# Two norms' right halves in a pipeline, and the gates among five pairs of products

## The chip, the cores and the metric

The kernel runs on one core of a Trainium2 chip. The engines of the core that matter here are TensorE (PE, matrix products), VectorE (DVE), ScalarE (ACT), GpSimd (POOL) and SyncE (SP, which starts the loads of weights). Each engine works through its own list of instructions in order, and waits where an instruction needs what another engine or a transfer has not yet delivered. The metric is the device time of one execution in microseconds (us).

## The reference

One layer of a diffusion backbone on 640 tokens (128 of context, 512 of latents) with 1024 channels: a SwiGLU half step, a mixer, a second half step, a last norm. Each of the first three stages begins with a norm that is modulated by channel, differently for the two token groups:

```python
def rmsnorm(x, g):
    y = x32 * lax.rsqrt(jnp.mean(x32 * x32, axis=-1, keepdims=True) + EPS)
    return (y * g.astype(jnp.float32)).astype(x.dtype)

    h = modulate(rmsnorm(x, norm_g[0]), sh1, sc1)
    x = x + 0.5 * g1[:, None, :] * swiglu(h, ffn1_w1, ffn1_w2)
    h = modulate(rmsnorm(x, norm_g[1]), shm, scm)
    y, C, n, m = mixer(h, ...)
    x = x + gm[:, None, :] * y
    h = modulate(rmsnorm(x, norm_g[2]), sh2, sc2)
    x = x + 0.5 * g2[:, None, :] * swiglu(h, ffn2_w1, ffn2_w2)
```

The mixer multiplies h by one wide matrix; of its columns come q, k, v, o, the mLSTM's input and forget gates, and two sets of merge gates. The mLSTM needs cumulated sums of log-sigmoids of the forget gates and running maxima, in both directions, before its first chunk:

```python
    z = h @ w_in + b_in
    ...
    b = jnp.cumsum(lfc, axis=-1)
    dmat = jnp.where(causal, b[..., :, None] - b[..., None, :] + ic[..., None, :], -jnp.inf)
    m_t = jnp.maximum(a, jnp.max(dmat, axis=-1))
    ...
    ml = (o * hm) @ w_ml_out
    sc = (bg * uc) @ w_sc_out
    y = jax.nn.sigmoid(z[..., GML_OFF:GSC_OFF]) * ml + jax.nn.sigmoid(z[..., GSC_OFF:IN_COLS]) * sc
```

## The kernel before, in words

**Products.** Everything is float32; a product of two float32 matrices is made of three products of reduced parts (`three`: high times high, high times low, low times high). Of each weight tile ACT makes the high part (wh, L73, a cast) and DVE the low part (wl, L74, a subtraction). The tokens lie in two halves of 320 columns, left and right. Most large products are done in *pairs* of 128 output rows by a scheme with seven products instead of eight (`pair_steps`). A pair's seven products P0 to P6 have 12 matmuls of 128x320 each. They need sums of weights (ws, L213, DVE) and combinations of the activations (H11, H12, HT1 to HT4 and so on). Between them stand small steps: a copy of the first bank by ACT after P0 (L268), copies by ACT after P1, P2 and P4 (L274, L278, L286), additions by DVE (L287 after P4, L292 after P5). P2 needs the copy L268, P4 needs L278, P6 needs L286, and the next pair's P1 needs L292 of this one. What a pair delivers last is handled late: it is flushed behind the next pair's L268.

**Norms two and three.** The norm stands ahead of a `head_el`: a loop over eight k steps in which three blocks of the left half are multiplied side by side (nine matmuls a step), followed by the three blocks' right half and the remaining blocks. The left half's rows are made while the stage before ends (`halves_el` and `left_lists`, seven lists of work that `after_lists` calls one by one). The right half's norm is made while the left half is multiplied: `chain[0]` is the statistics (the sum over channels of the squares, a matmul L719 of `sqacc` with ones; ACT's square root, DVE's reciprocal and three diagonals), `chain[1]` the spread of the result over all partitions by matmuls (L736), the scales of the eight rows (`scale_x`, L744, DVE) and the first four modulates (`modulate`, L752 on ACT or L754 on DVE in turn), `chain[2]` the other modulates and the splits (L73 cast by ACT, L74 subtraction by DVE) of the first four rows into HT4, `chain[3]` those of the last four into H22. Norm three's right half shares ACT with two silus of the second half step (L854), which need another table of functions.

**Gates.** After the first of the mixer's products, 38 steps of `gates()` (cumulated sums and maxima on DVE, exponentials and a logarithm on ACT, some transfers by POOL) and one step that opens buffers are dealt out evenly over pairs by `weave`: a step is put behind a product as soon as its share is reached. The four pairs are the last of v, the first of the merge gates gml (its results go through a sigmoid, L1516), and two of q and k. ACT holds one table of functions at a time, and where a function of another table follows, an ACT_TABLE_LOAD stands ahead of it.

**Later stages.** The other merge-gate pairs lie further on: gml's second pair among the first head's steps, its third and fourth beside the norm of the mLSTM's output, the four of gsc behind the ml stage.

Of the kernel before, what the change touches and what calls it, by code (L numbers as in the profile page):

```python
# [14 lines left out]
KT = 8  # L15
# [29 lines left out]
def mixer_step(ctx: ExitStack, tc: tile.TileContext, x_prompt, x_sample, state_C, state_n, state_m,  # L45
# [131 lines left out]
    def step(fn):  # L177
        return element([], [], fn)
# [147 lines left out]
    def plain_acts(k, h):  # L326
        if h == 0:
            return HB["11" if k < 4 else "21"][k % 4]
        return HB["12" if k < 4 else "22"][k % 4]

    def head_el(blocks, chain, work, mid=()):


        pre, nb = len(mid) // 2, len(blocks)
        order = [None] * pre + [0, 1, 2] + [None] * (len(mid) - pre) + list(range(3, nb))
        points = 4 * nb - 6
        at_ = {t: i for i, t in enumerate(order) if t is not None}

        def emit():
            flush()  # L340
            n = {"i": 0}

            def take(u, i):
                u["emit"](raw(el["base"] + i))
                rdone.add(el["base"] + i)
                load_more()

            def some(*_):
                n["i"] += 1
                if n["i"] == 3 and soon:  # L350
                    soon.pop(0)()
                while len(work) > 0 and n["i"] * total >= points * (total - len(work) + 1):
                    work.pop(0)()

            total = len(work)
            ev = lambda t: lambda h_, ps: blocks[t][1](h_, ps)
            hold()
            for i in range(pre):
                take(mid[i], i)
            w = [[op()] for t in range(3)]  # L360
            ps = [big() for t in range(3)]
            for k in range(KT):
                if k == 4:
                    for t in range(3):
                        w[t].append(op())
                for t in range(3):
                    three(ps[t][:, :HT], *w[t][k // 4], k % 4, plain_acts(k, 0), k == 0, k == KT - 1)
                if k == 3:
                    chain[0]()
                if k == 4:  # L370
                    chain[1]()
            for t in range(3):
                ev(t)(0, ps[t][:, :HT])
            chain[2]()
            for i in range(pre, len(mid)):
                take(mid[i], 3 + i)
            chain[3]()
            for t in range(3):
                unit(w[t], KT, plain_acts, 1, ev(t), {3: some, 7: some})
                release(2)  # L380
            for t in range(3, nb):
                w = [op(), op()]
                unit(w, KT, plain_acts, 0, ev(t), {3: some, 7: some})
                unit(w, KT, plain_acts, 1, ev(t), {3: some, 7: some})
            while work:
                work.pop(0)()
            for f in chain[4:]:
                f()
        loads = [b[0] for b in blocks]
        loads = [u["raws"][0] for u in mid[:pre]] + loads[:3] + [u["raws"][0] for u in mid[pre:]] + loads[3:]  # L390
        oa = [dict(tile_ops(KT, at_[t])[i], raws=[at_[t]]) for i in range(2) for t in range(3)]
        ob = [dict(o, raws=[at_[t]]) for t in range(3, nb) for o in tile_ops(KT, at_[t])]
        el = dict(element(loads, oa + ob, emit), calm=True)
        return el

# [382 lines left out]
    def right_chain(n, sh):  # L778

        def all_of(*fs):  # L780
            def f():
                for x in fs:
                    x()
            return f

        def scales():
            for k in range(KT):
                scale_x(1, k, N["rb", 1])

        def mods(ks):  # L790
            for k in ks:
                modulate(1, k, n, sh, "AV"[k % 2])

        def right(ks):
            for k in ks:
                if k < 4:
                    HB.setdefault("12", [None] * 4)[k] = hl = hpair("T4")
                    split(N[1, k], *hl)
                else:
                    put("22", k - 4, N[1, k])  # L800

        def t1(k):
            N["T", k] = utile()
            V.tensor_sub(N["T", k], N[1, k], N[0, k])

        def t2(k):
            V.tensor_sub(N["T", k], N[1, k + 4], N["T", k])

        def t3_(k):
            V.tensor_sub(N[1, k], N[1, k + 4], N[1, k])  # L810

        def t4(k):
            V.tensor_sub(N["T", k], N[0, k + 4], N["T", k])
        ks = range(4)
        work = [lambda k=k: t1(k) for k in ks] + [lambda k=k: put("T1", k, N["T", k]) for k in ks]
        work += [lambda k=k: t3_(k) for k in ks] + [lambda k=k: put("T3", k, N[1, k]) for k in ks]
        work += [lambda k=k: t2(k) for k in ks] + [lambda k=k: put("T2", k, N["T", k]) for k in ks]
        work += [lambda k=k: t4(k) for k in ks]
        last = [lambda k=k: put("T4", k, N["T", k]) for k in ks]
        chain = [stat_fn(1), all_of(rows_fn(1), scales, lambda: mods(range(4))),  # L820
                 all_of(lambda: mods(range(4, 8)), lambda: right(range(4))), lambda: right(range(4, 8))]
        return chain + last, work

    def add_x(m, h, ps, g, last):
# [56 lines left out]
    def after_lists(n, sh):  # L881
        lists = left_lists(n, sh)

        def after(h, i):
            if h == 1:
                for f in lists[i]:
                    f()
                if i == 5:
                    for f in lists[6]:
                        f()  # L890
        return after


# [628 lines left out]
    def cx_pair(m):  # L1522
        def ev(mi, h, src):
# [25 lines left out]
            for o, i in segs:  # L1549
# [7 lines left out]
    prog += [step(spill_x), step(close_u), step(open_h1)]  # L1557
    gate, NG = gates(), 38
    h1 = head_q(1)
    prog += weave([pair_el(*j, spare_v=True) for j in (h0[2], gml_pair(0), h1[0], h1[1])],  # L1560
                  [step(lambda: next(gate, None))] * NG + [step(open_ml)])
    for h in range(NH):
        o_pair = q_pair(h, "o", O_OFF)
        if h == 0:
            jobs = [gml_pair(2), h1[2], o_pair]
        elif h + 1 < NH:
            jobs = head_q(h + 1) + [o_pair]
        else:
            jobs = [cx_pair(0), o_pair, cx_pair(1)]
        prog += weave([pair_el(*j) for j in jobs], head_steps(h))  # L1570
# [114 lines left out]
    rs += [n_out, lambda: None, open_m2]  # L1685
    rs += [lambda j=j: (r_in(j)(), r_load(j + 3)() if j + 3 < KT else None) for j in range(KT)]
    rs = [step(f) for f in rs]
    prog += weave([pair_el(*gml_pair(m), spare_v=True) for m in (4, 6)], rs)
    ml = [plain_el(w_load(w_ml_out, 0, KT, m * P, D), KT, lambda k, h: RB[k, h], ml_ev(m)) for m in range(KT)]
    for m in range(KT):  # L1690
        ml[m]["fill"] = [step(g_load(m + 1))] if m + 1 < KT else []
# [2 lines left out]
    for m in range(0, KT, 2):  # L1694
        if m:
            prog += [pair_el(*cx_pair(m), G), pair_el(*cx_pair(m + 1), G)]
        prog.append(pair_el(*bg_pair(m), G, spare_v=True))
    prog += weave([pair_el(*gsc_pair(m)) for m in range(0, KT, 2)], [step(lambda: None)] * 3 + [step(t_in(0))])
    y_acts = lambda k, h: YB[k, h]
    sc = [plain_el(w_load(w_sc_out, 0, KT, m * P, D), KT, lambda k, h: PB[k, h], sc_ev(m)) for m in range(KT)]  # L1700
    for m in range(KT - 1):
# [102 lines left out]
```

## Time and profile before

| | |
|---|---|
| median of 3 runs | 1712.4 us (1710.86 to 1714.94) |
| profiled execution | 1714.5 us |
| its span on the core | 1712.7 us |
| granted TensorE clock, mean | 0.994 |
| busy: PE, DVE, ACT, POOL | 1673.4, 1269.8, 798.3, 166.5 us |
| pairs of the gates | 541 to 591 us |
| norm two's right half | 501 to 520 us |
| norm three's right half | 1256 to 1277 us |

A row of the profile's time line gives the start in us, the duration, the engine, the line and the operation, output and inputs, and in brackets how long the engine stood idle just before and who released it. A row of the windows gives busy us of each engine in the stretch, then PE's granted clock and the share and rate of the transfers. The matmul durations overlap: one starts about every 0.15 us though each is listed with 0.31.

### The profile page before, as it was taken

How to read it: one execution, taken by the hardware profiler on the slowest of the kernel's cores; microseconds unless marked ns; L12 is line 12 of the kernel's file. 1: busy time of each engine (PE TensorE's matmuls, PEld its weight loads, DVE VectorE, ACT ScalarE, POOL GpSimd, SP SyncE). 2: the span in 40 equal slices, each digit the busy share in tenths (PEclk: the TensorE clock that was granted, in tenths of full speed). 3: DMA queues.
4: the chain of work that ended last, by engine and by line, in shares of the span. 5: the costliest groups of instructions: out<-in, count | busy, mean ns of one | idle time of the engine just before them, and what ended most of it. 6: DMA issues, size and time to landing. Idle time of an engine off the chain costs nothing.

```text
span 1712.7 us, 29519 instructions
## 1 busy us (share of the span) xinstructions
PE 1673.4 (98%) x11269; PEld 1625.6 (95%) x11269; DVE 1269.8 (74%) x2684; ACT 798.3 (47%) x1719; POOL 166.5 (10%) x250
## 2 busy tenths in 40 slices
PE   7999999999999899999999999999999999999997
PEld 4989999999989899999999999999989999999997
DVE  6767786886778867777887788879677567566576
ACT  4542451542456666465662355542265335244253
POOL 2010000000030231111111221011100000000002
PEclk9999999999999999999999999999999999999999
DMA  9344334333352443333348433357432322323222
GB/s 310 86 144 140 99 109 118 110 112 108 102 159 75 107 105 84 84 100 83 95 144 270 120 83 83 96 167 214 123 99 65 96 62 84 90 74 90 84 74 62
DMA packets 278349, 193.14 MB, mean 113 GB/s; under 512 B 12291, under 2 KB 256650, under 8 KB 278208
## 3 DMA queue, kind: packets, MB, share of 16 engines
q1 hardware_dynamic: 268960, 161.96, 32.8%
q0 software_dynamic: 8480, 28.63, 5.9%
q8 instruction: 89, 1.46, 0.3%
q10 hardware_dynamic: 768, 0.66, 0.1%
q14 instruction: 52, 0.43, 0.1%
HBM read 175.92 MB, written 15.31 MB: 112 GB/s over the span
## 4 chain that ended last, share of the span: by engine, by line
PE 83%; DVE 8%; ACT 5%; issue 3%; DMA 1%; POOL 0%; ACTq 0%; DVEq 0%; POOLq 0%
PE ps L240 25%; PE ps L242 25%; PE ps L241 25%; DVE wl L74 2%; PE ax L1385 1%; PE ax L1416 1%; ACT wh L73 1%; PE ax L636 1%; PE ax L1388 1%; PE ax L561 1%; DVE ws L213 1%; DVE t L1529 1%; DMA wr<-in_ffn_w_dram 0%; DVE x L1541 0%; PE ax L1362 0%
## 5 line engine op out<-in xcount | busy, mean ns | idle before, releaser
L74 DVE TENSOR_TENSOR wl<-wr,wh 128x512 fp32r<-128x512 f32 (+1 forms) x410 | 266.9, 666 | 81.1 <-ACT wh L73 79.5
L73 ACT CAST wh<-wr 128x512 fp32r<-128x512 f32 (+1 forms) x410 | 238.7, 593 | 181.3 <-PE ps L241 152.5
L74 DVE TENSOR_TENSOR wl<-ws,wh 128x512 fp32r<-128x512 f32 x288 | 203.0, 705 | 62.4 <-ACT wh L73 62.0
L73 ACT CAST wh<-ws 128x512 fp32r<-128x512 f32 x288 | 175.2, 618 | 111.6 <-DVE ws L213 65.9
L240 PE MATMUL ps<-Uh,wh 128*128 128x320 f32 x704 | 218.5, 310 | 0.0
L241 PE MATMUL ps<-Ul,wh 128*128 128x320 f32 x704 | 217.3, 309 | 0.0
L242 PE MATMUL ps<-Uh,wl 128*128 128x320 f32 x704 | 217.2, 308 | 0.0
L828 DVE SCALAR_TENSOR_TENSOR x<-ps,modT,x 128x128 f32<-128x128 f32 (+2 forms) x216 | 82.7, 433 | 121.1 <-PE ps L242 121.1
L241 PEld LDWEIGHTS ps<-Ul,wh 128*128 128x128 f32 x704 | 132.1, 188 | 0.2 <-DVE Ul L74 0.2
L240 PEld LDWEIGHTS ps<-Uh,wh 128*128 128x128 f32 x704 | 132.1, 188 | 0.0
L242 PEld LDWEIGHTS ps<-Uh,wl 128*128 128x128 f32 x704 | 132.1, 188 | 0.0
L240 PE MATMUL ps<-HT4h,wh 128*128 128x320 f32 x384 | 122.4, 319 | 8.5 <-DVE t L289 3.5
L240 PE MATMUL ps<-H11h,wh 128*128 128x320 f32 x384 | 121.1, 315 | 2.0 <-ACT H11h L73 2.0
L240 PE MATMUL ps<-H21h,wh 128*128 128x320 f32 x384 | 120.3, 313 | 1.2 <-ACT H21h L73 1.2
L241 PE MATMUL ps<-HT4l,wh 128*128 128x320 f32 x384 | 119.8, 312 | 0.2
L242 PE MATMUL ps<-HT4h,wl 128*128 128x320 f32 x384 | 119.6, 312 | 0.0
L241 PE MATMUL ps<-H11l,wh 128*128 128x320 f32 x384 | 119.0, 310 | 0.6 <-DVE H11l L74 0.4
L242 PE MATMUL ps<-H21h,wl 128*128 128x320 f32 x384 | 119.1, 310 | 0.3
L241 PE MATMUL ps<-H21l,wh 128*128 128x320 f32 x384 | 118.7, 309 | 0.1
L242 PE MATMUL ps<-H11h,wl 128*128 128x320 f32 x384 | 118.6, 309 | 0.0
L240 PE MATMUL ps<-H22h,wh 128*128 128x320 f32 x352 | 110.6, 314 | 0.0
L242 PE MATMUL ps<-H22h,wl 128*128 128x320 f32 x352 | 109.1, 310 | 0.0
(399 smaller groups left out, 4531.1 us busy)
## 6 DMA issues: line engine op xcount, KB each, us to landing
wr<-in_ffn_w_dram SPq DMA_DIRECT2D x86, 512.0 KB, 3.9
wr<-in_w_in_dram SPq DMA_DIRECT2D x72, 512.0 KB, 3.9
wr<-in_w_mod_dram SPq DMA_DIRECT2D x64, 512.0 KB, 4.0
wr<-in_ffn_w_dram SPq DMA_DIRECT2D x48, 384.0 KB, 3.5
wr<-in_ffn_w_dram SPq DMA_DIRECT2D x20, 256.0 KB, 3.0
early<-in_w_mod_dram SPq DMA_DIRECT2D x8, 512.0 KB, 9.1
wr<-in_w_ml_out_dram SPq DMA_DIRECT2D x8, 512.0 KB, 5.1
wr<-in_w_sc_out_dram SPq DMA_DIRECT2D x8, 512.0 KB, 4.2
```

Of the source, the lines that this page charges most:

```text
L73: A.copy(hi, raw)
L74: V.tensor_sub(lo, raw, f32(hi))
L213: getattr(engine, fn)(t, part(o, a), part(o, b))
L240: PE.matmul(ps, hi[:, ws], ah, start=start, stop=False, skip_group_check=True)
L241: PE.matmul(ps, hi[:, ws], al, start=False, stop=False, skip_group_check=True)
L242: PE.matmul(ps, lo[:, ws], ah, start=False, stop=stop, skip_group_check=True)
L561: PE.matmul(S["p"][g, c:c + n], cm[:, k, :], w[:, n * j:n * j + n], start=(k < 4), stop=(k >= 4), skip_group_check=True, tile_position=(0, ...
L636: PE.matmul(p[:, 2 * j + i:2 * j + i + 1], hold_[i][j * P // n][:, a:a + P], ones[:, 0:1], start=True, stop=True)
L828: V.scalar_tensor_tensor(X[m][:, o + a:o + b], ps[:, a:b], modT[:, g, m, cd:cd + 1], X[m][:, o + a:o + b], op0=OP.mult, op1=OP.add)
L1385: PE.matmul(p2[:, :DH + 1], S["q", dt][:, sl], S["C"][d][:, dt, :], start=(dt == 0), stop=(dt == 1))
L1388: PE.matmul(p1[:, :DH + 1], S["p", ch][:, d, :], PO["vt"][:, ch, :], start=True, stop=True)
L1416: PE.matmul(p[:, :DH + 1], kw[:, dt * P:(dt + 1) * P], PO["vt"][:, ch, :], start=True, stop=True)
```

## The change

Two things. In norms two and three, the right half's statistics are issued behind the second k step (k = 1) instead of the fourth, and the last list of the left half, which the stage before used to run at its end, is kept back and runs behind them. The spread follows after k = 3 instead of k = 4. The rows are then made in a pipeline, in which the scale of row k, the modulate of row k-1 and the split of row k-2 are issued in turn; all modulates of the right half go to ACT. In the gates, the 39 steps lie among five pairs: gml's second pair joins the four. The later gml pairs each move one place forward, and the first of gsc moves to the place that gml's last held.

```diff
                 for t in range(3):
                     three(ps[t][:, :HT], *w[t][k // 4], k % 4, plain_acts(k, 0), k == 0, k == KT - 1)
+                if k == 1:
+                    chain[0]()
+                    for f in N.pop("rest"):
+                        f()
                 if k == 3:
-                    chain[0]()
-                if k == 4:
                     chain[1]()
...
-        def scales():
-            for k in range(KT):
-                scale_x(1, k, N["rb", 1])
-
-        def mods(ks):
-            for k in ks:
-                modulate(1, k, n, sh, "AV"[k % 2])
...
+        def rows(k0, k1):
+
+            for k in range(k0, k1):
+                if k < KT:
+                    scale_x(1, k, N["rb", 1])
+                if 1 <= k <= KT:
+                    modulate(1, k - 1, n, sh)
+                if k >= 2:
+                    right(k - 2)
...
-        chain = [stat_fn(1), all_of(rows_fn(1), scales, lambda: mods(range(4))),
-                 all_of(lambda: mods(range(4, 8)), lambda: right(range(4))), lambda: right(range(4, 8))]
+        chain = [stat_fn(1), all_of(rows_fn(1), lambda: rows(0, 6)), lambda: rows(6, 9), lambda: rows(9, 10)]
...
                 if i == 5:
-                    for f in lists[6]:
-                        f()
+                    N["rest"] = lists[6]
...
-    prog += weave([pair_el(*j, spare_v=True) for j in (h0[2], gml_pair(0), h1[0], h1[1])],
+    prog += weave([pair_el(*j, spare_v=True) for j in (h0[2], gml_pair(0), gml_pair(2), h1[0], h1[1])],
                   [step(lambda: next(gate, None))] * NG + [step(open_ml)])
...
-            jobs = [gml_pair(2), h1[2], o_pair]
+            jobs = [gml_pair(4), h1[2], o_pair]
...
-    prog += weave([pair_el(*gml_pair(m), spare_v=True) for m in (4, 6)], rs)
+    prog += weave([pair_el(*j, spare_v=True) for j in (gml_pair(6), gsc_pair(0))], rs)
...
-    prog += weave([pair_el(*gsc_pair(m)) for m in range(0, KT, 2)], [step(lambda: None)] * 3 + [step(t_in(0))])
+    prog += weave([pair_el(*gsc_pair(m)) for m in range(2, KT, 2)], [step(lambda: None)] * 3 + [step(t_in(0))])
```

On DVE in norm two, from the last diagonal (dg) of the right half's statistics on, the list before has all scales (Ul and Uh from x), then two modulates; the left half's splits (H21l) stand ahead of it:

```order
L729 TENSOR_SCALAR dg_5901<-ident_91,rstd_5894 128x128
L744 TENSOR_TENSOR Ul_5916<-x_141,ax_5912 128x320
L744 TENSOR_TENSOR Uh_5918<-x_142,ax_5912 128x320
L744 TENSOR_TENSOR Ul_5920<-x_143,ax_5912 128x320
L744 TENSOR_TENSOR Uh_5922<-x_144,ax_5912 128x320
L744 TENSOR_TENSOR Ul_5924<-x_145,ax_5912 128x320
L744 TENSOR_TENSOR Uh_5926<-x_146,ax_5912 128x320
L744 TENSOR_TENSOR Ul_5928<-x_147,ax_5912 128x320
L744 TENSOR_TENSOR Uh_5930<-x_148,ax_5912 128x320
L754 TENSOR_SCALAR Uh_5918<-Uh_5918,gcol_134,modT_133 128x320
L754 TENSOR_SCALAR Uh_5922<-Uh_5922,gcol_134,modT_133 128x320
```

Now three of the left half's splits (H21l) stand behind the diagonals (dg), and splits of the first right rows (HT4l) stand between the scales:

```order
L731 TENSOR_SCALAR dg_5869<-ident_91,rstd_5862 128x128
L74 TENSOR_TENSOR H21l_5874<-Uh_5740,H21h_5873 128x320
L74 TENSOR_TENSOR H21l_5878<-Ul_5742,H21h_5877 128x320
L74 TENSOR_TENSOR H21l_5882<-Uh_5767,H21h_5881 128x320
L746 TENSOR_TENSOR Ul_5907<-x_141,ax_5903 128x320
L746 TENSOR_TENSOR Uh_5909<-x_142,ax_5903 128x320
L746 TENSOR_TENSOR Ul_5912<-x_143,ax_5903 128x320
L74 TENSOR_TENSOR HT4l_5916<-Ul_5907,HT4h_5915 128x320
L746 TENSOR_TENSOR Uh_5919<-x_144,ax_5903 128x320
L74 TENSOR_TENSOR HT4l_5923<-Uh_5909,HT4h_5922 128x320
L746 TENSOR_TENSOR Ul_5926<-x_145,ax_5903 128x320
L74 TENSOR_TENSOR HT4l_5930<-Ul_5912,HT4h_5929 128x320
```

The four modulates of the right half that DVE had are gone from this list; they stand on ACT.

On ACT in the gates, before, around the exponentials (L1266 to L1276) that follow the running maxima; ps is a bank of a product, row_wi and row_wk are rows of the gates, x takes the results of q:

```order
L278 COPY ps_6767<-ps_6702 128x320
L1266 ACT_TABLE_LOAD
L1266 ACTIVATE sm_de_6677<-sm_de_6677 36x5
L1268 ACTIVATE row_s_6421<-row_s_6421 36x640
L73 CAST wh_6773<-wr_6404 128x512
L1309 ACTIVATE x_6789<-ps_6683,biT_132 128x320
L1274 ACTIVATE row_wi_6747<-row_f_6376,sm_mi_6674 36x128
L73 CAST wh_6796<-ws_6771 128x512
L286 COPY t3_6812<-ps_6767 128x320
L1276 ACTIVATE row_wk_6746<-row_i_6375,sm_nl_6676 36x128
L1274 ACTIVATE row_wi_6747<-row_f_6376,sm_mi_6674 36x128
```

The same place now, with gml's second pair (L1517, the sigmoid) between:

```order
L1267 ACT_TABLE_LOAD
L1267 ACTIVATE sm_de_6766<-sm_de_6766 36x5
L1269 ACTIVATE row_s_6421<-row_s_6421 36x640
L73 CAST wh_6854<-ws_6831 128x512
L268 COPY ps_6870<-ps_6851 128x320
L1517 ACT_TABLE_LOAD
L1517 ACTIVATE t3_6872<-ps_6737,biT_132 128x320
L1517 ACTIVATE t3_6875<-t3_6790,biT_132 128x320
L1275 ACT_TABLE_LOAD
L1275 ACTIVATE row_wi_6829<-row_f_6376,sm_mi_6763 36x128
L73 CAST wh_6882<-ws_6852 128x512
L274 COPY t3_6900<-ps_6881 128x320
```

A pair's late sigmoids now fall between two exponentials, behind the copy L268 and ahead of L274 and L278, with a table load on either side; ACT's list has 24 table loads instead of 22.

On DVE in the ml stage, before, a product's preparation (x from wr and cm) waits for two transfers:

```order
L74 TENSOR_TENSOR wl_11042<-wr_11032,wh_11041 128x512 [waits DMAHW6_49,Activation_49]
L74 TENSOR_TENSOR wl_11046<-wr_11032,wh_11045 128x512 [waits Activation_49]
L625 TENSOR_SCALAR x_11069<-wr_10892,cm_93 128x512 [waits DMAHW3_49,DMASW6_49]
L627 SCALAR_TENSOR_TENSOR x_11069<-wr_10892,cm_93,x_11069 128x512 [waits DVE_49]
L625 TENSOR_SCALAR x_11090<-wr_10892,cm_93 128x512 [waits DMASW0_49]
L627 SCALAR_TENSOR_TENSOR x_11090<-wr_10892,cm_93,x_11090 128x512 [waits DVE_49]
```

Now the same pair of instructions waits for one transfer and for PE:

```order
L74 TENSOR_TENSOR wl_11184<-wr_11174,wh_11183 128x512 [waits DMAHW0_49,Activation_49]
L74 TENSOR_TENSOR wl_11188<-wr_11174,wh_11187 128x512 [waits Activation_49]
L627 TENSOR_SCALAR x_11211<-wr_11034,cm_93 128x512 [waits DMAHW5_49,PE_49]
L629 SCALAR_TENSOR_TENSOR x_11211<-wr_11034,cm_93,x_11211 128x512 [waits DVE_49]
L627 TENSOR_SCALAR x_11232<-wr_11034,cm_93 128x512 [waits PE_49]
L629 SCALAR_TENSOR_TENSOR x_11232<-wr_11034,cm_93,x_11232 128x512 [waits DVE_49]
```

The x buffer that it takes was last read by a reduction on PE, since two more tiles are taken ahead of the stage.

More of the change, by code (lines that the diff above doesn't have):

```diff
@@ L784, in all_of, with right @@
             return f
-        def scales():
-            for k in range(KT):
-                scale_x(1, k, N["rb", 1])
-        def mods(ks):
-            for k in ks:
-                modulate(1, k, n, sh, "AV"[k % 2])
[L794 to L800, printed above, removed]
+        def right(k):
+            if k < 4:
+                HB.setdefault("12", [None] * 4)[k] = hl = hpair("T4")
+                split(N[1, k], *hl)
+            else:
+                put("22", k - 4, N[1, k])
+        def rows(k0, k1):
[6 more added lines that the diff above has]
+                    right(k - 2)
         def t1(k):
```

## The prediction

> **What bounds the kernel now.** I read the page first, then windows of one pair each around the gates, then PE's, DVE's and ACT's time lines at the three places that the change touches.
>
> ```profile
> PE 1673.4 (98%) x11269; PEld 1625.6 (95%) x11269; DVE 1269.8 (74%) x2684; ACT 798.3 (47%) x1719; POOL 166.5 (10%) x250
> ...
> 541.50:553.80 12.30, 12.27 (x84) 12.01 (x83) 9.99 (x22) 6.85 (x13) 0.00 (x0) 1.00 0.32 87
> 553.80:566.10 12.30, 11.17 (x75) 10.64 (x73) 11.55 (x18) 8.87 (x15) 2.02 (x6) 1.00 0.31 83
> 566.10:578.40 12.30, 8.22 (x52) 7.70 (x53) 11.75 (x30) 5.71 (x12) 2.78 (x6) 1.00 0.16 50
> 578.40:590.70 12.30, 12.30 (x85) 12.10 (x84) 9.11 (x15) 11.11 (x27) 5.24 (x9) 1.00 0.81 164
> ```
>
> PE is busy in 98% of 1712.7 us, so only some 39 us of idle time can be won. The windows (busy us of PE, PEld, DVE, ACT, POOL) show 5.2 us of it in the two middle pairs of the gates, where DVE has 11.55 and 11.75 of 12.30 us. The order lists of PE and SP have as many rows after the change as before, so no product and no load is added; the change is worth what PE waits more or less at the two norms, the gates and the ml stage.
>
> **Norm two.** PE, then DVE and ACT:
>
> ```profile
> 501.15 0.41 PE L240 MATMUL ps<-H11h,wh 128*128 128x320 f32 x1 [1.54 <-ACT H11h L73]
> 506.09 0.28 PE L719 MATMUL ax<-ones,sqacc 128*128 128x2 f32 x2
> 508.90 0.91 PE L736 MATMUL ax<-dg,ones 128*128 128x128 f32 x6
> 515.82 0.41 PE L240 MATMUL ps<-HT4h,wh 128*128 128x320 f32 x1 [1.05 <-ACT HT4h L73]
> 516.35 0.41 PE L241 MATMUL ps<-HT4l,wh 128*128 128x320 f32 x1
> 519.81 0.31 PE L240 MATMUL ps<-HT4h,wh 128*128 128x320 f32 x1
> ...
> 503.15 0.49 DVE L714 TENSOR_TENSOR sqacc<-sqacc,t 128x320 f32<-128x320 f32 x1 [0.67 <-ACT t L713]
> 509.84 0.49 DVE L744 TENSOR_TENSOR Ul<-x,ax 128x320 f32<-128x320 f32 x1 [0.70 <-PE ax L736]
> 513.03 0.80 DVE L754 TENSOR_SCALAR Uh<-Uh,gcol,modT 128x320 f32<-128x320 f32 x2
> ...
> 514.23 1.19 ACT L752 ACTIVATE Ul<-Ul,modT,gcol 128x320 f32<-128x320 f32 x2
> 515.32 0.44 ACT L73 CAST HT4h<-Ul 128x320 fp32r<-128x320 f32 x1
> ```
>
> The statistics matmul (L719) stands at 506.09, though its operand, the last sum of squares, is ready at 503.15+0.49 = 503.64. All eight scales follow the spread (first at 509.84), then the modulates, then the splits, so the first right row HT4h comes at 515.8 and the first right-half unit of 24 matmuls ends where the next begins, at 519.81. Between 516.35 and 519.81 lie 23.6 spacings, that is 0.147 each: a unit is 3.5 us, a k of three blocks (nine matmuls) 1.32 us, a product (twelve) 1.757 us, a pair (seven products) 12.3 us.
>
> After the change the statistics come behind k=1, which runs from 501.15 to about 502.95 (1.32 and restarts), so at 503.68: PE waits 0.7 for the sum, a wait that before does not have (bounds 0 and 1.0). The statistics take 0.6, two steps of products take PE to 506.9. Square root, reciprocal and three diagonals took the 2.8 us between 506.09 and 508.90 or less; the kept-back left rows (a modulate, three splits) stand behind the diagonals on DVE, but the square root stands ahead of them. I put the spread at 507.29, a wait of 0.35. First scale: 507.29+0.91 = 508.2, against 509.84. Then scale, modulate and split overlap: DVE does about 0.40 + 0.40 per row (half of the 0.80 of two), ACT about 0.55 (from 514.23 to 515.32 are two) and 0.36 for the cast, so rows come every 0.91 us and the first four are there before PE has ended the left half. That end stays the bound: 507.95 + 4 x 1.32 = 513.3, then the modulation matmuls, and the unit starts at 514.4 and ends at 518.2 with 0.3 for restarts. **Gain 1.6 us.** The cover is gone if ACT's four further modulates (4 x 0.55 = 2.2 us) arrive last; then gain 0. At best both waits vanish: 2.0.
>
> **Norm three** has a further ACT load before the last rows.
>
> ```profile
> 1258.41 0.49 DVE L714 TENSOR_TENSOR sqacc<-sqacc,t 128x320 f32<-128x320 f32 x1 [0.67 <-ACT t L713]
> ...
> 1261.34 0.39 PE L719 MATMUL ax<-ones,sqacc 128*128 128x2 f32 x3
> 1271.74 0.41 PE L240 MATMUL ps<-HT4h,wh 128*128 128x320 f32 x1 [1.74 <-ACT HT4h L73]
> 1277.29 0.31 PE L240 MATMUL ps<-HT4h,wh 128*128 128x320 f32 x1
> ...
> 1268.21 1.28 ACT L854 ACT_TABLE_LOAD   x1 [1.14 <-PE ps L242]
> 1269.50 0.77 ACT L854 ACTIVATE t<-ps 128x320 f32<-128x320 f32 x2
> ...
> 1274.00:1278.00 4.00, 4.00 (x21) 4.00 (x21) 2.23 (x6) 0.67 (x3) 0.00 (x0) 0.69 0.14 33
> ```
>
> The sum is ready at 1258.41 + 0.49, so the statistics move from 1261.34 to 1258.95, the spread follows 3.6 later as in norm two and the first scale another 0.91 later, at 1263.46. On ACT six rows end 4.88 us later, the table load and two silus (1.28 + 0.65) at 6.85 us, then two modulates and four splits; the last right row is complete at 10.75 us, so the unit ends at 1263.46 + 11.1 = 1274.56, against 1277.29: **2.7 us**. Of this 1.5 us is not the order's: the unit takes 1277.29 - 1271.74 = 5.55 us, where norm two's takes 519.81 - 515.82 = 3.99, and the granted clock is 0.69 in the window from 1274. A run without this lost clock gains 1.2.
>
> **Gates.** Waits of PE, then DVE's stretch, then ACT:
>
> ```profile
> 541.28 0.39 PE L240 MATMUL ps<-H11h,wh 128*128 128x320 f32 x1
> 558.31 0.41 PE L240 MATMUL ps<-HT2h,wh 128*128 128x320 f32 x1 [0.65 <-ACT ps L268]
> 567.45 0.41 PE L240 MATMUL ps<-HT4h,wh 128*128 128x320 f32 x1 [1.84 <-ACT t L286]
> 572.90 0.42 PE L240 MATMUL ps<-HT1h,wh 128*128 128x320 f32 x1 [1.66 <-DVE t L292]
> 575.98 0.41 PE L240 MATMUL ps<-HT2h,wh 128*128 128x320 f32 x1 [1.06 <-ACT ps L268]
> ...
> 555.41 0.69 DVE L74 TENSOR_TENSOR wl<-wr,wh 128x512 fp32r<-128x512 f32 x1 [0.54 <-ACT wh L73]
> 556.02 0.81 DVE L1198 SCALAR_TENSOR_TENSOR row_e<-row_s,row_e 36x640 f32<-36x640 f32 x1
> 578.86 0.81 DVE L1264 TENSOR_TENSOR row_s<-row_l,row_f 36x640 f32<-36x640 f32 x1
> ...
> 548.66 0.53 ACT L1309 ACTIVATE v<-ps,biT 128x320 f32<-128x320 f32 x1 [0.86 <-ACT wh L73]
> 549.21 1.28 ACT L1190 ACT_TABLE_LOAD   x1
> 550.50 0.74 ACT L1190 ACTIVATE row_e<-row_e 36x640 f32<-36x640 f32 x1
> 575.51 0.42 ACT L268 COPY ps<-ps 128x320 f32<-128x320 f32 x1
> 575.86 0.52 ACT L1516 ACTIVATE t<-ps,biT 128x320 f32<-128x320 f32 x1
> 580.39 0.72 ACT L1268 ACTIVATE row_s<-row_s 36x640 f32<-36x640 f32 x1
> ```
>
> Up to 572.90 DVE's list holds PE up by 0.65 + 1.84 + 1.66 = 4.15 us, 5.2 with the restarts (the first pair starts at 541.28, and 15 products of 1.757 later it would be 567.6). DVE's stretch without a gap, 555.41 to 578.86, is 23.45 us: ten weight remainders and five sums (0.60 each, as from 555.41 to 556.02), two adds (0.9) and so 13.5 of gate steps. With five pairs there are 1.1 steps to a product instead of 1.4. The Ln stands two products later (14.13 us after the first pair's start becomes about 18.05), and from there to the L292 of gml's second pair DVE has 12 remainders and 6 sums, four adds and the same gate steps: 10.8 + 1.6 + 13.5 = 25.9, up to 43.95. The next pair's second product, which needs that L292, could begin unhindered at 3 x 12.3 + 1.76 = 38.66 and so begins 5.3 us late: the stretch is longer by the work of the added pair and as late as before. **DVE part 0** (bounds: 0.8 gained, if the remainders overlap more of the Ln's wait; 1.0 lost).
>
> ACT is new. Gml's second pair now leaves late sigmoids behind the next pair's L268, between exponentials, so two table loads (1.28 each) are added. From L292 on ACT does sigmoid, cast, table load, two exponentials, cast and the copy L268 (0.47 + 0.52 + 1.29 + 0.11 + 0.63 + 0.52 + 0.35) and ends at 47.8, while the product before ends at 45.7: P2 waits 2.2 us. Then table load, two sigmoids, table load, exponentials, casts and a copy (5.8 us) until L278 at 53.6, while P3 ends at 51.4: P4 waits 2.3. Both together stand against the 1.06 of before: **3.4 us lost**. Lower end: 0, if the table loads fall into ACT's idle time; upper: 6.5.
>
> These sums take the next ACTIVATE to start as the load ends: 549.21 begins as the sigmoid before it ends (548.66 + 0.53) and 550.50 follows 1.29 later. The Trainium skill ("ScalarE: Activation LUTs", section "What ACT_TABLE_LOAD costs") says that a switch of table costs about 1283 ns of load and about 1380 ns of drain; the trace agrees on the load and shows no drain.
>
> **ml stage.**
>
> ```profile
> 934.13 0.49 DVE L625 TENSOR_SCALAR x<-wr,cm 128x512 f32<-128x512 f32 x1 [2.88 <-DMA td<-x]
> 943.78 0.93 DVE L1617 TENSOR_TENSOR x<-ps,x 128x320 f32<-128x320 f32 x2 [3.41 <-PE ps L242]
> ```
>
> Tiles shift in the x buffers, so DVE's L625 now waits for a reduction on PE instead of a DMA. DVE, with weight remainders behind it, would stand still up to 5 us, of which 2.88 were idle already and the rest meets the 3.41 of idle time near it. I take 0 (bounds 0 and 5, as PE waits only when the cover of some seven us of prepared weights is used up). The gate DMA of POOL that now precedes its memsets has no reader on the path: 0.
>
> **Sum.** -1.6 - 2.7 + 0 + 3.4 = -0.9 against the profiled 1714.5, giving 1713.6; against the median 1712.4, whose runs I take to be without the lost clock, -1.6 - 1.2 + 3.4 = +0.6, giving 1713.0. I forecast 1713.3, between the two.
>
> **Rivals.**
> - *The table loads are hidden.* For it: ACT is busy 47% overall. Against: 11.11 of 12.30 us in the window 578.40. Then 1.06 is won too: -1.6 - 2.7 - 1.1 = -5.4 from 1714.5, 1709.1, or -3.9 from 1712.4, 1708.5; between them 1708.8, which is just over 0.2% faster. Chance 0.17.
> - *Slower by the clock.* The two new idle stretches of 2.2 and 2.3 us each lose the clock as the 1.74 did at 1271.74 (1.5 us each): 1713.3 + 3.0 = 1716.3. Against: the waits of 1.84 and 1.66 kept the clock at 1.00. It decides once one window is lost with norm three gaining 1.2. Chance 0.13. "TensorE: Matmul & The Clock Gate" of the Trainium skill, Part 1, has the clock halved after an idle window of about 3.4 us; the stretch of half clock here fits that length, the 1.74 us wait before it is shorter.
> - *Table loads cost twice.* If ACT stood a second 1.28 us at each of three new loads of the chain, 3.8 more: 1717.1. Chance 0.05, since 550.50 shows none. That is what the drain rule of the Trainium skill above would make of it.
> - *The ml stage's cover fails*: up to 5, 1718. Chance 0.05.
>
> **How the numbers follow.** What a measurement can tell from no change is about 0.2%, 3.4 us. The forecast has 0.55, and lies within it; another 0.05 is for losses at the norms (ACT's modulates late). Faster by more: 0.17; slower: 0.13 + 0.05 + 0.05 + 0.05 = 0.28; same 0.55. The range from 1708.8 (loads hidden) to 1717.3 (clock or drain) leaves two in ten out.
>
> **What would show it.** Norm two: statistics near 503.7, first right unit with a wait under 0.5. Norm three: the last silus ahead of the last splits, unit end near 1274.6. Gates: two more table loads and two waits over 2 us, released by ACT L268 and L278, and DVE full over three pairs. Wrong, if those waits are missing, or DVE's stretch makes another wait than 5.3, or PE waits at the ml stage for wl.

## The result, and the profile after

The changed kernel is slower: 1718.6 us in the median of 15 runs (1714.0 to 1721.2) against 1712.4 before (15 runs). The ratio is 1.0035, with a 95% interval of 1.0027 to 1.0042, so about 6.0 us (4.6 to 7.2) are lost where 0.9 were forecast. The profiled execution took 1719.8 us, its span is 1718.0. The page's first line, with the share of PE as before, shows why the page alone does not help here:

```profile
PE 1675.9 (98%) x11269; PEld 1627.9 (95%) x11269; DVE 1269.5 (74%) x2676; ACT 806.1 (47%) x1730; POOL 167.2 (10%) x250
```

PE is even *longer* busy, by 2.5 us, with as many instructions: a matmul at half clock counts as busy. I therefore laid the matmuls of both traces side by side, the n-th with the n-th, and read the shift at the borders of the stages. From start to end the changed trace falls 5.3 us behind:

| stage | shift, us | forecast |
|---|---|---|
| start, before any changed instruction | -1.9 (a stretch of half clock that this execution lacks) | 0 |
| norm two | +0.8 | -1.6 |
| gates, five pairs, less a later pair of 12.7 | +4.0 | +3.4 |
| heads, and the two pairs beside the mLSTM's output norm | about +4.8 | 0 |
| ml stage | 0.0 | 0 |
| norm three | -2.4 | -2.7 |

**Norm two**, PE's time line, then windows with the granted clock (third number from the end):

```profile
499.25 0.42 PE L240 MATMUL ps<-H11h,wh 128*128 128x320 f32 x1 [1.56 <-ACT H11h L73]
501.80 1.44 PE L721 MATMUL ax<-ones,sqacc 128*128 128x2 f32 x6
507.74 0.83 PE L738 MATMUL ax<-dg,ones 128*128 128x128 f32 x6
...
500.00:504.00 4.00, 3.87 (x17) 3.47 (x17) 3.27 (x9) 3.32 (x9) 2.49 (x5) 0.57 1.07 381
504.00:508.00 4.00, 4.00 (x19) 4.00 (x19) 2.50 (x8) 1.78 (x5) 0.00 (x0) 0.58 1.01 373
```

The wait of 1.05 us on HT4h is gone, as forecast, and the rows are ready in time. But from 500.5 to 507.4 the clock is at half: the two windows lose 0.43 x 4 + 0.42 x 4 = 3.4 us. The half clock begins before the statistics, and PE waits for the sum of squares for only 0.13 us, where 0.7 were forecast, because the products ahead of it already run slowly. For the same reason the spread comes 5.9 us behind the statistics, not 3.6.

**Gates**, PE's waits, then ACT from the table load to the copy L278, then one window:

```profile
564.95 0.42 PE L240 MATMUL ps<-HT4h,wh 128*128 128x320 f32 x1 [1.12 <-ACT t L286]
570.20 0.41 PE L240 MATMUL ps<-HT1h,wh 128*128 128x320 f32 x1 [1.47 <-DVE t L292]
572.97 0.42 PE L240 MATMUL ps<-HT2h,wh 128*128 128x320 f32 x1 [0.75 <-ACT ps L268]
581.52 0.42 PE L240 MATMUL ps<-HT4h,wh 128*128 128x320 f32 x1 [0.74 <-ACT t L286]
589.16 0.55 PE L240 MATMUL ps<-HT2h,wh 128*128 128x320 f32 x1 [2.05 <-ACT ps L268]
595.13 0.41 PE L240 MATMUL ps<-HT3h,wh 128*128 128x320 f32 x1 [0.65 <-ACT ps L278]
...
586.15 1.28 ACT L1267 ACT_TABLE_LOAD   x1
587.45 0.21 ACT L1267 ACTIVATE sm_de<-sm_de 36x5 f32<-36x5 f32 x1
587.56 0.72 ACT L1269 ACTIVATE row_s<-row_s 36x640 f32<-36x640 f32 x1
588.69 0.41 ACT L268 COPY ps<-ps 128x320 f32<-128x320 f32 x1
589.13 1.28 ACT L1517 ACT_TABLE_LOAD   x1
591.41 1.28 ACT L1275 ACT_TABLE_LOAD   x1
594.66 0.41 ACT L278 COPY ps<-ps 128x320 f32<-128x320 f32 x1
...
588.00:592.00 4.00, 2.84 (x11) 2.84 (x12) 0.69 (x1) 3.95 (x7) 2.10 (x4) 0.66 0.90 61
```

Here the forecast can be read step by step. The wait for L268 is 2.05 us (2.2 was forecast). Of the second wait, 2.3, only 0.65 shows, because the two products before it ran at half clock and ended 1.7 us later: what the clock took, the wait gave back. Waits and lost clock together are 4.4 us, against 4.5.

**Beside the mLSTM's output norm** there is what the forecast did not have, two waits of PE, the ACT casts behind them, and again a window of half clock:

```profile
906.99 0.41 PE L240 MATMUL ps<-HT2h,wh 128*128 128x320 f32 x1 [0.65 <-ACT ps L268]
916.60 0.41 PE L240 MATMUL ps<-HT4h,wh 128*128 128x320 f32 x1 [1.80 <-ACT t L286]
...
905.27 0.82 ACT L73 CAST Bh<-x 128x320 fp32r<-128x320 f32 x2 [1.11 <-DMA rd<-o]
914.89 0.82 ACT L73 CAST Bh<-x 128x320 fp32r<-128x320 f32 x2 [2.23 <-DMA x<-rd]
916.13 0.41 ACT L286 COPY t<-ps 128x320 f32<-128x320 f32 x1
...
916.00:920.00 4.00, 3.40 (x14) 3.40 (x15) 3.16 (x7) 2.59 (x7) 1.07 (x2) 0.62 0.79 263
```

ACT's casts of the mLSTM's rows (Bh) wait for rows that come back from memory, and the copies of the pair (L268, L286) stand behind them in ACT's list.

**Norm three** went as forecast: ACT does the table load and the silus after five modulates and four casts, and PE starts the right half without a wait. The first unit ends at 1282.57, which is 1274.9 on the clock of the trace before (7.68 less, the shift at that place), where 1274.6 was forecast. The unit itself takes 5.47 us, about as long as before (5.55): then a stretch of half clock made it long, now PE stops several times for the last four rows.

```profile
1277.10 0.41 PE L240 MATMUL ps<-HT4h,wh 128*128 128x320 f32 x1
1282.57 0.31 PE L240 MATMUL ps<-HT4h,wh 128*128 128x320 f32 x1
...
1276.25 1.28 ACT L856 ACT_TABLE_LOAD   x1
1277.54 0.77 ACT L856 ACTIVATE t<-ps 128x320 f32<-128x320 f32 x2
```

### The profile page after: what moved, and what is told of

It is laid out like the page before. It is cut to its first block, busy times and chain, and to the rows that moved or that the text cites. A ratio compares the mean times of both kernels' runs of the same rounds, so it can differ in the third digit from the quotient of the medians.

```text
span 1718.0 us, 29528 instructions
## 1 busy us (share of the span) xinstructions
PE 1675.9 (98%) x11269; PEld 1627.9 (95%) x11269; DVE 1269.5 (74%) x2676; ACT 806.1 (47%) x1730; POOL 167.2 (10%) x250
## 3 DMA queue, kind: packets, MB, share of 16 engines
q8 instruction: 89, 1.46, 0.4%
## 4 chain that ended last, share of the span: by engine, by line
PE 81%; DVE 8%; ACT 5%; issue 3%; DMA 2%; POOL 0%; ACTq 0%; DVEq 0%; POOLq 0%
PE ps L240 25%; PE ps L241 25%; PE ps L242 25%; DVE wl L74 2%; PE ax L1386 1%; ACT wh L73 1%; PE ax L1417 1%; PE ax L638 1%; PE ax L1389 1%; DVE ws L213 1%; DVE t L1530 1%; PE ax L563 1%; DMA wr<-in_ffn_w_dram 0%; DVE x L1542 0%; PE ax L1363 0%
## 5 line engine op out<-in xcount | busy, mean ns | idle before, releaser
L241 PE MATMUL ps<-H22l,wh 128*128 128x320 f32 x352 | 109.3, 311 | 0.4
```

Source lines behind the costliest of these rows:

```text
L241: PE.matmul(ps, hi[:, ws], al, start=False, stop=False, skip_group_check=True)
```

## The experiments

All kernels ran beside the kernel before on the same chip, whose median was 1712.3, 1711.8 or 1711.3 us there; ratios are to it. "Below the changed kernel" compares medians with its 1718.6; where the ratios give another distance, it stands beside it.

### The norms alone

The changed kernel with the lists of pairs put back:

```diff
-    (h0[2], gml_pair(0), gml_pair(2), h1[0], h1[1])
+    (h0[2], gml_pair(0), h1[0], h1[1])
...
-            jobs = [gml_pair(4), h1[2], o_pair]
+            jobs = [gml_pair(2), h1[2], o_pair]
...
-    prog += weave([pair_el(*j, spare_v=True) for j in (gml_pair(6), gsc_pair(0))], rs)
+    prog += weave([pair_el(*gml_pair(m), spare_v=True) for m in (4, 6)], rs)
```

> The norms' part alone; gates and the places of the merge-gate pairs as before. Theory A (the parts add, and the norms' pipeline gains what the waits say): 1.6 to 2.4 us faster at each of the two norms, so 3 to 4.5 us faster than the kernel before, about 1708.5, with no new wait outside the norms. Rival B (the early statistics cost norm two its clock each time, as the profile of the changed kernel shows 3 us at a granted clock of 0.5 to 0.66 there): only 0 to 1.5 us faster, about 1711.5, and the half-clock stretch near 500 us is there again.

1710.3 us (11 runs), ratio 0.9990 (0.9981 to 0.9999): 1.7 us faster (0.2 to 3.3). The waits at the norms went as in the changed kernel; its profile has the half clock at norm two too, for 6.8 us from 497.86 on. PE's rows, then windows with the granted clock:

```profile
500.44 1.27 PE L721 MATMUL ax<-ones,sqacc 128*128 128x2 f32 x6
896.03 0.41 PE L240 MATMUL ps<-HT4h,wh 128*128 128x320 f32 x1 [1.60 <-ACT t L286]
...
494.45:497.86 3.41, 1.85 (x14) 1.50 (x10) 1.21 (x4) 2.77 (x7) 2.15 (x4) 1.00 0.95 306
497.86:501.27 3.41, 3.33 (x14) 3.13 (x13) 2.68 (x8) 2.29 (x7) 2.98 (x6) 0.50 1.07 355
501.27:504.69 3.42, 3.42 (x15) 3.42 (x15) 3.38 (x10) 2.87 (x8) 0.00 (x0) 0.50 1.02 410
```

The time lies between theories A and B, and is lower than that of the changed kernel and of the kernel before. Two rows matter later. The clock falls 2.6 us before the statistics, and PE does not wait for the sum of squares at all here. And beside the mLSTM's output norm, where this kernel has gml's pairs as before, there is a wait of 1.60 us for L286.

### The gates alone

```diff
-    prog += weave([pair_el(*j, spare_v=True) for j in (h0[2], gml_pair(0), h1[0], h1[1])],
+    prog += weave([pair_el(*j, spare_v=True) for j in (h0[2], gml_pair(0), gml_pair(2), h1[0], h1[1])],
...
-            jobs = [gml_pair(2), h1[2], o_pair]
+            jobs = [gml_pair(4), h1[2], o_pair]
...
-    prog += weave([pair_el(*gml_pair(m), spare_v=True) for m in (4, 6)], rs)
+    prog += weave([pair_el(*j, spare_v=True) for j in (gml_pair(6), gsc_pair(0))], rs)
```

> The gates' part alone: five pairs in the gates, gml's last and gsc's first pair beside the mLSTM's output norm; norms as before. Theory A: the gates cost about 4 us and the place beside the output norm about 4 us (waits of 2.7 us and one lost clock window), so 7 to 9 us slower than before, about 1720. Rival C (the gates alone carry the loss, the other place is chance): about 4 us slower, 1716.5, and no wait over 1 us between 900 and 925 us.

1718.6 us (6 runs), ratio 1.0035 (1.0023 to 1.0047): the whole loss lies in this part, which holds the five pairs of the gates and the move beside the output norm. The gates' waits are those of the changed kernel to 0.03 us each; beside the output norm the waits for the pair's copies are 1.5 us instead of 2.7, and no window is lost there in this execution. The two parts alone add up to +4.3, the whole change measured +6.0; with intervals of about 1.5 us each the difference is not settled.

### gsc's results through memory

```diff
+            if m == 0:
+                t = t3()
+                A.activation(t, src, AF.Sigmoid, bias=bias(GSC_OFF + (m + mi) * P))
+                G.dma_start(gsd[m + mi][:, hsl(h)], t)
+                return
...
+    [step(gs_load(0)), step(gs_load(1)), step(lambda: None), step(t_in(0))]
```

> The changed kernel, but the results of gsc's first pair go through memory and are loaded into x buffers only where gsc's first pair stood before, so that the tail has all its x buffers for the mLSTM's rows. Theory A (two x buffers held by gsc's results make the loads of these rows late, which holds ACT's casts and the copy L286): the waits of 0.65 and 1.80 us near 907 and 917 us go, no ACT cast there waits over 1 us for a transfer, and the time is 3 to 4 us below the changed kernel, about 1715. Rival D (the wait comes from gsc's sigmoids or the order of the pairs itself): the wait of 1.8 us stays, same time within 1 us.

1717.2 us (6 runs), ratio 1.0027 (1.0016 to 1.0039), 1.4 below the changed kernel, which is within the intervals. The last wait fell from 1.80 to 0.33 us, the first rose from 0.65 to 1.62:

```profile
594.05 0.42 PE L240 MATMUL ps<-HT3h,wh 128*128 128x320 f32 x1 [2.19 <-ACT ps L278]
908.25 0.41 PE L240 MATMUL ps<-HT2h,wh 128*128 128x320 f32 x1 [1.62 <-ACT ps L268]
916.38 0.41 PE L240 MATMUL ps<-HT4h,wh 128*128 128x320 f32 x1 [0.33 <-ACT t L286]
...
590.00:594.00 4.00, 1.87 (x13) 1.60 (x11) 0.98 (x2) 3.97 (x9) 1.63 (x3) 1.00 0.90 245
594.00:598.00 4.00, 3.94 (x16) 3.95 (x17) 3.06 (x6) 2.78 (x9) 0.94 (x2) 0.57 0.64 190
```

So theory A fails for the first wait. For the last one the fall is no sign for it either: with gsc's results in the x buffers that wait was 1.80 us in the changed kernel and 0.73 in the gates alone, and of the next two runs, one has no such wait over 0.15 us and the other 0.20. The uppermost row is from the gates: here the clock stayed full until 594, and the second wait in the gates is 2.19 us, the 2.3 of the forecast; the window is then lost behind it.

### gml's second pair as the last of the five

```diff
-    (h0[2], gml_pair(0), gml_pair(2), h1[0], h1[1])
+    (h0[2], gml_pair(0), h1[0], h1[1], gml_pair(2))
```

> The changed kernel with gml's second pair as the last of the five gate pairs, so that its sigmoids come after all exponentials; 23 table loads instead of 24, none between the exponentials. Theory A (the two table loads between exponentials make the wait of 2.05 us before L268 and part of the later 0.65 us): these waits go and the time is 2 to 4 us below the changed kernel, about 1715.5. Rival E (DVE's stretch, which has the same work, makes the waits): the sum of PE's waits in the gates stays at 7 us within 1, and the time within 1 us.

1714.7 us (11 runs), ratio 1.0019 (1.0010 to 1.0028), 3.9 below the changed kernel (2.7 by the ratios). There are still 24 table loads, but the two behind L268 are gone and with them the wait for L278. But the wait for L268 is as long as it was:

```profile
585.88 0.42 PE L240 MATMUL ps<-HT2h,wh 128*128 128x320 f32 x1 [2.04 <-ACT ps L268]
...
584.00:588.00 4.00, 2.12 (x12) 2.12 (x13) 1.41 (x3) 3.99 (x11) 0.54 (x1) 0.91 0.85 158
588.00:592.00 4.00, 4.00 (x21) 4.00 (x20) 2.91 (x6) 2.65 (x7) 0.91 (x2) 0.66 0.63 169
```

My theory of this wait, that the loads *between* the exponentials make it, fell; what stands ahead of L268 in both lists is the first load of the exponentials' table. The next run moves that.

### The first exponentials two products later

```diff
+        yield
+        yield
         A.activation(de, de, AF.Exp)
         yield
         A.activation(en, en, AF.Exp, scale=-1.0)
...
-            yield
+            if ch not in (1, 3):
+                yield
```

> The changed kernel with the first two exponentials of the gates (and with them the table load) two products later, behind the copy L268 and the late sigmoids, so that ACT does sigmoid, cast, L268, sigmoids and one table load: 22 loads as before, and the wait of 2.05 us should not be there. Theory F (the load and two exponentials ahead of L268 make that wait, and a wait of 2 us there costs a clock window of 1.7 us, as in four of four profiles with it): PE's waits between 540 and 612 us fall from 7.3 to about 5, no half clock there, and the time is 3 to 5 us below the changed kernel's 1718.6, about 1714.5. Rival E (DVE's stretch sets the wait): the wait before L268 stays over 1.5 us and the time within 1.5 us.

1714.1 us (11 runs), ratio 1.0012 (1.0003 to 1.0021), 4.5 below the changed kernel (3.9 by the ratios). PE's and ACT's rows and the windows:

```profile
587.08 0.42 PE L240 MATMUL ps<-HT2h,wh 128*128 128x320 f32 x1 [0.37 <-ACT ps L268]
591.80 0.42 PE L240 MATMUL ps<-HT3h,wh 128*128 128x320 f32 x1 [0.93 <-ACT ps L278]
...
586.60 0.42 ACT L268 COPY ps<-ps 128x320 f32<-128x320 f32 x1
587.95 1.28 ACT L1269 ACT_TABLE_LOAD   x1
...
584.00:588.00 4.00, 3.63 (x25) 3.33 (x24) 3.77 (x7) 2.98 (x7) 2.48 (x4) 1.00 0.23 48
588.00:592.00 4.00, 3.07 (x21) 2.81 (x20) 1.24 (x2) 3.99 (x9) 2.56 (x5) 1.00 0.92 83
```

The wait of 2.05 is 0.37, the clock stays at 1.00, and the time falls by what theory F gave. Since the late sigmoids now come before the exponentials, one table load stands where three stood. The table loads' place and number are the larger part of the change's loss, 3.9 of 6.0 us. The waits behind DVE's stretch (1.13, 1.47, 0.76, 0.76) are unchanged; PE's waits in the gates sum to 5.9 us, still above the 5.2 of four pairs. Five pairs win nothing on DVE.

### Each norm alone

The new form in norm two only (1 in the condition), and in norm three only (2); the other as before.

```diff
-                    N["rest"] = lists[6]
+                    if n == 1:
+                        N["rest"] = lists[6]
+                    else:
+                        for f in lists[6]:
+                            f()
...
+        if n != 1:
+            chain = [stat_fn(1), all_of(rows_fn(1), scales, lambda: mods(range(4))),
+                     all_of(lambda: mods(range(4, 8)), lambda: rights(range(4))), lambda: rights(range(4, 8))]
```

> The norms' part in norm two alone; norm three and all the rest as before. Theory G (norm two wins 1 us of waits and loses as much or more to the clock, since the early statistics stand within one window of the wait of 1.56 us): -1 to +1.5 us against before, about 1712.5. Theory A (both norms gain by their waits): 1.6 us faster, 1710.7.

1712.6 us (11 runs), ratio 1.0000 (0.9992 to 1.0009).

> The norms' part in norm three alone. Theory G (norm three's wait of 1.74 to 2.05 us always cost a clock window, two of two profiles with the old norm, none of four with the new, so all the gain lies here): 2.4 to 3.2 us faster than before, about 1709.5, faster than both parts together (1710.3). Theory A: 1.2 to 2.4 us faster, slower than both together.

1710.9 us (11 runs), ratio 0.9993 (0.9984 to 1.0002). Norm two gains nothing: its 1.0 us of waits is given back in windows like these of the first of the two kernels:

```profile
499.95 0.41 PE L240 MATMUL ps<-H11h,wh 128*128 128x320 f32 x1 [1.56 <-ACT H11h L73]
502.50 0.37 PE L724 MATMUL ax<-ones,sqacc 128*128 128x2 f32 x1 [0.42 <-DVE sqacc L719]
...
500.00:504.00 4.00, 3.47 (x16) 2.84 (x17) 3.27 (x9) 2.88 (x8) 3.18 (x7) 0.70 1.06 363
504.00:508.00 4.00, 4.00 (x16) 4.00 (x17) 3.20 (x9) 2.48 (x7) 0.00 (x0) 0.50 1.02 383
```

Theory G's time is right for norm two, and so is the half clock that it expected there. Norm three's share, 1.2 us with an interval from 2.7 faster to 0.3 slower, is less than G said, and does not beat both norms together; whether it is as large as the trace's 2.4 the runs don't tell.

### The move beside the output norm alone

```diff
-            jobs = [gml_pair(2), h1[2], o_pair]
+            jobs = [gml_pair(2), gml_pair(4), h1[2], o_pair]
...
-    prog += weave([pair_el(*gml_pair(m), spare_v=True) for m in (4, 6)], rs)
+    prog += weave([pair_el(*j, spare_v=True) for j in (gml_pair(6), gsc_pair(0))], rs)
```

> Only the move beside the mLSTM's output norm: gml's last and gsc's first pair there, gml's third among the first head's steps (four pairs instead of three), gates and norms as before. Theory A (less x buffers): PE's waits between 870 and 960 us rise from 1.1 to 2.5 or more, and the time by 1.5 to 3 us, about 1714.5. Rival D (the waits there come from the time that the mLSTM's rows need through memory, whichever pairs lie there): 1 us either way of 1712.3.

1713.9 us (11 runs), ratio 1.0012 (1.0003 to 1.0021), but in the profile not for the reason asked: most of it is a new wait among the first head's four pairs, with its window.

```profile
622.50 0.64 PE L240 MATMUL ps<-HT3h,wh 128*128 128x320 f32 x1 [2.21 <-ACT ps L278]
902.60 0.42 PE L240 MATMUL ps<-HT2h,wh 128*128 128x320 f32 x1 [0.49 <-ACT ps L268]
```

The waits beside the output norm are 1.5 us, 0.4 more than before. So this run is no clean answer on the tail. What the traces do show: the wait for L268 near 905 us is there in all six kernels with gsc's pair in that place (0.65, 0.51, 1.62, 1.25, 1.64, 0.49) and in none of the five with gml's (before, the norms alone in two forms, either norm alone). Why the first rows come back later there stays open; the x buffers are not it, by the run with gsc's results in memory. The wait for L286 is no mark of the move: it is 1.80 us in the changed kernel, but also 1.60 in the norms alone, which does not have the move.

### Norm two's statistics one step later

```diff
-                if k == 1:
+                if k == at_k[0]:
                     chain[0]()
...
-                if k == 3:
+                if k == at_k[1]:
                     chain[1]()
...
-                        mod_mid(GM, 0)))
+                        mod_mid(GM, 0), (2, 4)))
```

> Both norms' pipelines, gates as before, but in norm two the statistics stand behind k = 2 and the spread behind k = 4, so that PE does not wait for the sum of squares. Theory G (in norm two the second wait of 0.6 us, soon after the one of 1.56, is what brings the clock windows lost there): no wait on sqacc in norm two, 0 to 1.7 us at half clock there instead of 3.4, and 1 to 2 us faster than the norms' part as it stands, about 1709. Rival H (the wait of 1.56 alone, with the short matmuls ahead of it, makes them; the statistics don't matter): the half clock stays as often as with the old norm (1.3 us in the mean of four profiles) or more, and the time is within 1 us of 1710.3.

1709.7 us (11 runs), ratio 0.9987 (0.9978 to 0.9996), 2.2 us faster than before: the fastest of all. PE does not wait for the sum of squares, and the rows are in time all the same; one window is lost in this profile, 1.7 us.

```profile
498.27 0.41 PE L240 MATMUL ps<-H11h,wh 128*128 128x320 f32 x1 [1.56 <-ACT H11h L73]
502.94 0.39 PE L721 MATMUL ax<-ones,sqacc 128*128 128x2 f32 x3
...
500.00:504.00 4.00, 4.00 (x23) 4.00 (x22) 3.22 (x8) 3.04 (x9) 1.49 (x3) 0.71 1.03 403
```

Against the norms as they stood it is 0.6 us, within both theories' reach, and one lost window in one profile is within both too. Neither tells G from H.

## Why the prediction was wrong

The forecast was 1713.3, with 0.28 for slower; the measured 1718.6 lies above the range.

- **"-1.6" at norm two: right about the wait on HT4h, but the gain is 0.** That wait went and the rows came in time. What failed is that the sum counts the steps behind the statistics at full clock and has no term for a clock that falls there. The six profiles with the new norm two lost 3.4, 3.4, 1.7, 0, 3.4 and 3.4 us to half clock, the four with the old one 0, 1.7, 1.7 and 1.7. That is 1.3 us more in the mean, for 1.0 of waits won. The first lost window stands behind the wait of 1.56 that the old form has too. The second is there in the four profiles in which the statistics begin inside the first, and in none of the four in which they come after it. The wait for the sum of squares, theory G's cause, is not what the profiles show: where 3.4 us were lost it is 0, 0, 0.13 and 0.42 us, where 1.7 and 0 were lost it is 0.59 and 0.58. Whether the statistics' six short matmuls (128x2, 1.3 us at half clock) keep the clock down was not tried.
- **"-2.7", or "-1.2" for a run without the lost clock, at norm three: right in the trace.** The trace moved by 2.4. From the first scale (1271.29) the last right row took 10.8 us for the 10.75 forecast. The second half of the step was an error: I took median runs to have no lost clock there. Three of the four profiles with the old norm three lost 1.7 us there, and none of the seven with the new one. Alone it measured 1.2, with a wide interval.
- **"DVE part 0": right.** DVE's stretch, whose first and last rows follow, runs from 558.85 to 585.0 in the trace after, 26.2 us for the 25.9 forecast (the sum gives four adds 1.6 us, where it gives two 0.9; with 1.8 it would be 26.1), and ends 44.9 us after the first pair's start (540.15) for 43.95.

```profile
558.85 0.69 DVE L74 TENSOR_TENSOR wl<-ws,wh 128x512 fp32r<-128x512 f32 x1 [2.02 <-ACT wh L73]
...
584.55 0.47 DVE L292 TENSOR_TENSOR t<-ps,t 128x320 f32<-128x320 f32 x1
```

- **"3.4 us lost" on ACT: right as a sum, with one part under another name.** The pairs took 4.0 us more. (The two ends in the forecast, 47.8 and 45.7, are 2.1 apart, not 2.2.) Waits of 2.05 and 0.65 and a lost window of 1.7 stand for the two waits of 2.2 and 2.3. The rival of the clock added 1.5 us for each on top of the waits; one window is lost in four of four profiles (the changed kernel and the runs of the gates alone, gsc through memory and gml last), and where it falls ahead of the second wait, it is hidden in that. Its argument against itself, that waits of 1.84 and 1.66 us kept the clock, did not hold for waits of 2 us.
- **"I take 0" beside the output norm and the ml stage: the step that failed most in the trace.** I followed the x buffers into the ml stage, where nothing happened (the shift stays at 7.68 us through it), and put no price on the place that gsc's first pair moves to. There, waits rose from 1.1 to 3.5 us in the profiled execution, and a window was lost. How much of this the move costs stays open: the five other kernels with it wait 1.5 to 3.0 us there and lose no window, and four kernels without it wait 0.8, 1.1, 1.1 and 2.4 us. Only the wait for L268 (0.5 to 1.6 us) is there with the move alone, and its cause is open. An estimate from the times is 2 us: 6.0 for gates and tail, less the 4.0 of the five pairs in the trace.
- **The rival "table loads cost twice" fell.** In the trace after, the load at 589.13 follows L268's end (588.69 + 0.41), and the load at 586.15 ends where the exponential starts, 1.30 us later at 587.45. The drain of about 1380 ns that the Trainium skill ("ScalarE: Activation LUTs", section "What ACT_TABLE_LOAD costs") states is in neither trace.

Together: gates and tail 6 us (measured alone, 3.9 to 8.0) where 3.4 were counted, norms 1.7 where 2.8 to 4.3 were.

## What to carry to other kernels

When work moves, price the place that receives what was displaced, not only the place that was meant: here the last pair of a chain of moves landed beside a stage that waits on memory, and at no price. A table load belongs behind the copy that the matrix engine waits for: with the first load two products later, and one load where there were three, the kernel won about 4 us. And a wait of the matrix engine near 2 us costs more than itself: in three of four profiles the wait of 2.05 us for L268 took another 1.7 us of clock, so such a wait should be priced at up to 3.7 us.

## What the hardware showed that was not expected

The lost clock comes in pieces: stretches of half clock of 3.413 us, or two of them in a row, in every place and profile where PE ran on both sides, and each loses half of that, 1.71 us. The Trainium skill ("TensorE: Matmul & The Clock Gate", Part 1) has the same length, a free-running window of 3413 ns, and the traces agree on that. It says that the clock falls after an idle window; here much less is enough.

The stretches lie on a grid. In the trace after, half clock begins at 97.76, 500.53, 589.28 and 916.96 us: 118, 26 and 96 times 3.413 us apart. In the other traces, too, the stretches begin whole multiples of it apart, so the borders between windows can be counted on to every wait:

| wait of PE | profiles | longest part inside one window, us | lost in the window behind it, us |
|---|---|---|---|
| 2.04 to 2.06, gates, L268 | 4 | 2.02 to 2.06 in three, 1.69 in one | 1.7 in the three, 0 in the one |
| 2.19, gates, L278 (gsc through memory) | 1 | 2.19 | 1.7 |
| 2.21, first head, L278 | 1 | 2.13 | 1.7 |
| 1.80, beside the output norm, L286 | 1 | 1.80 | 1.7 |
| 1.74, norm three before | 4 | 1.74 in three, 1.12 in one | 1.7 in the three, 0 in the one |
| 1.83 to 1.85, gates, L286 | 6 | 0.96 to 1.57 | 0 in all |
| 1.65 to 1.67, gates, L292 | 6 | 1.66 or 1.67 in five, 1.46 in one | 0 in all |
| 1.54 to 1.56, norm two, old and new | 11 | all of it in ten, 1.40 in one | 1.7 in eight of the ten, 0 in three (one of these loses the window after it) |

So it is not the length of a wait alone that decides, but how much of it lies in one window. The waits of 1.84 us in the gates kept the clock in all six profiles, and a border cuts each of them: in the trace before it lies at 566.50, so that 0.88 us fall into one window and 0.96 into the next. Counted over all eleven traces (between 40 and 1690 us), each of the 11 windows in which PE stood 1.74 us or more was followed by half clock. Of the 14 windows with 1.64 to 1.69 us, seven were, all at norm two; of the 52 with 1.0 to 1.63, one was. Below 1.0 there is a single one, with 0.86 us and the statistics' six matmuls in it (norm two, gsc through memory). What tells norm two from the gates at the same idle time stays open. The short matmuls of L563 just ahead of its wait, whose rows show 128*32 in place of 128*128, are not it: in seven of the eight cases they lie in the window before.
